# A hybrid encoder trunk: the attention and HGRN steps of its mixer are placed anew, and the Newton step of its inverse roots moves from VectorE to GpSimd

## The chip, the cores and the metric

The kernel runs on one core of a Trainium2 chip. What counts is the device time of one execution in microseconds (us). The engines are named as the profile names them: PE is TensorE (PEld its weight loads), DVE is VectorE, ACT is ScalarE, POOL is GpSimd and SP is SyncE, which here only issues DMAs. Each engine works through its own queue in order and waits on semaphores for the others.

## The reference

A two-layer trunk over 1024 tokens of width 1024, in float32. Layer 0 has a mixer of two head groups that share an input projection; layer 1 has a convolution module; each layer ends with a squared-ReLU MLP of width 4096, and an RMS norm stands before every block and at the end.

```python
u = rmsnorm(h, norm_mix_g[layer])
if layer % 2 == 0:
    h = h + parallel_ab_mixer(u, ...)      # stick-breaking attention (8 heads x 64) beside HGRN2 (4 heads x 128),
                                           # concatenated, one output projection
else:
    h = h + conformer_conv(u, ...)         # GLU, causal depthwise conv of width 31, LayerNorm, swish, pointwise
h = h + squared_relu_mlp(rmsnorm(h, norm_ffn_g[layer]), w_ff1[layer], w_ff2[layer])

# attention, per head: key_pos < q_pos
z = q @ k.T * scale;  log_beta = log_sigmoid(z);  log_keep = where(mask, log_beta - z, 0)
w = where(mask, exp(log_beta + cumsum_after(log_keep)), 0);  out = w @ v

# HGRN2, per head: f = lb + (1 - lb) * sigmoid(f_raw)
S_t = diag(f_t) S_{t-1} + (1 - f_t) i_t^T;  o_t = S_t^T q_t;  out = rmsnorm(o) * norm_g * silu(gate)

def rmsnorm(x, g):
    return x * rsqrt(mean(x * x) + 1e-6) * g
```

## The kernel before

The activations are kept transposed, channels on partitions and tokens along the free dimension, and are worked on in two halves of 512 tokens (`hf` 0 and 1, or a and b). A weight panel is 128 output channels by 1024 inputs: `panel` loads it by SP (`wraw`, two buffers) and splits it into a high part (ACT, line 104) and a low part (DVE, line 105); `gemm` then issues 24 matmuls of 128x512 for it (lines 115 to 117), three for each of eight input tiles, as high-high, high-low and low-high.

**The mixer's order is written by hand.** `TOKENS` lists the projection panels in order; each takes one place, from 0 up, except the tokens L, X, B, S and N, which take none. In the list, v, qk, f, q, i and g with a number and a half are projections; B loads the second half's input and S is its norm; X loads the residual `ht`; L4 and its like load one finished 128-channel block of the mixer's output back from DRAM on ACT's queue (`load_o`, into a `wraw` buffer); o0 to o7 are the output projection panels of the first half; N is the norm before the first MLP (`first_norm`); each m is one panel of that MLP. `A_SPANS` gives for each attention head the stretch of places over which its first and its second half's steps are spread evenly, and `G_SPANS` does so for the HGRN halves (entry 4 is head 2's first half, called 2a, entry 5 is 2b, entry 6 is 3a). `spread` sorts all steps by place and emits them in that order.

The emitted order is a priority, not yet the order on an engine: the framework's scheduler simulates the program and gives each engine the ready instruction of the highest priority. `tc.high_priority` puts panels' splits and evictions (`PRIO`) and the statistics (`SPRIO`) ahead. From there the order on each engine is fixed.

**An attention half** (`attn`) consists of `begin` (split of v), for each 128 queries `weights` (score matmuls with `kd` and `kl`, a sigmoid on ACT into `ke`, the mask on GpSimd at line 364, and a running product on DVE at line 367), for each pair of key blocks `apply` (transposes at line 380, a high/low split into `wt` on ACT and DVE at lines 384 and 385, and the product with v at line 389), and `end`, which writes the block to DRAM. A first half has nine steps and a second half thirteen. `ke` has three buffers, `wt`, `qs` and `kd` two or three, and the PSUM tags z, tr and av two each.

**An HGRN half** (`hg`) has seven steps: `gates` (a DVE scan, a reciprocal at line 460 and products), `level0` and two `level` steps, `state`, `output` (whose squares go through `stats`) and `finish`.

**`stats`** turns column sums of squares into 1/sqrt broadcast over partitions. TensorE sums (line 126), then a mean plus epsilon `m` is formed (line 129), GpSimd raises it to the power -0.5 (line 131), a Newton step refines it (lines 133 to 135), the result is split into high and low (137, 138), TensorE broadcasts it (`stb`, line 142) and ACT copies it out (144). It is called 21 times: for the norms, for the eight HGRN halves and for the LayerNorms.

After the mixer the rest of the second half's output projection, the MLPs, the convolution (31 taps on DVE, line 768) and layer 1 follow, with panels of the MLP interleaved with whatever DVE works on.

Of the kernel before, what the change touches and what calls it, by code (L numbers as in the profile page):

```python
# [8 lines left out]
F32 = mybir.dt.float32  # L9
F32R = mybir.dt.float32r  # L10
BF16 = mybir.dt.bfloat16
AF = mybir.ActivationFunctionType
ALU = mybir.AluOpType
# [14 lines left out]
TOKENS = (  # L28
# [4 lines left out]


A_SPANS = [
    (4, 7, 9.5, 12.5), (3, 8, 13, 13.2), (17, 18, 18, 20), (18.5, 21, 24, 29.5), (33, 33.2, 33.7, 35.5),
    (35, 36.5, 36.5, 36.7), (47, 48.5, 52, 66.5), (48.5, 48.7, 63, 74.5)
]
G_SPANS = [
    (4.5, 8), (18, 21.5), (23, 28), (28.5, 34.5), (38, 40), (49.5, 49.7), (40, 44), (65, 78)  # L40
]
GF = 8
XW = 2
# [10 lines left out]
def kernel(  # L54
# [13 lines left out]
    PE, ACT, DVE, POOL = nc.tensor, nc.scalar, nc.vector, nc.gpsimd  # L68
# [50 lines left out]
    def stats(pool, tag, src, count, eps, dst):  # L119

        n = dst.shape[-1] // P
        with tc.high_priority(offset=SPRIO):
            ps = pool.tile([P, H], F32, tag=tag, name="st")
            for c in range(n):
                for i, x in enumerate(src):
                    PE.matmul(ps[:, 2 * c:2 * c + 2], x[:, c * P:(c + 1) * P], ones[:, 0:2],  # L126
                              start=i == 0, stop=i == len(src) - 1, skip_group_check=True)
            m = tp.tile([P, 4], F32, tag="st_m", name="st_m")[:, :n]
            DVE.tensor_scalar(m, ps[:, 0:2 * n:2], 1.0 / count, eps, ALU.mult, ALU.add)
            r = tp.tile([P, 4], F32, tag="st_r", name="st_r")[:, :n]  # L130
            POOL.tensor_tensor(r, m, nhalf[:, :n], ALU.pow)
            t = tp.tile([P, 4], F32, tag="st_t", name="st_t")[:, :n]
            DVE.tensor_tensor(t, r, r, ALU.mult)
            DVE.scalar_tensor_tensor(t, t, -0.5, m, ALU.mult, ALU.mult)
            DVE.scalar_tensor_tensor(r, t, 1.5, r, ALU.add, ALU.mult)
            rr = tp.tile([P, 2, 4], F32R, tag="st_rr", name="st_rr")[:, :, :n]
            DVE.tensor_copy(rr[:, 0], r)
            DVE.tensor_tensor(rr[:, 1], r, rr[:, 0].bitcast(F32), ALU.subtract)
            pb = pool.tile([P, H], F32, tag=tag, name="stb")
            for c in range(n):  # L140
                for i in range(2):
                    PE.matmul(pb[:, c * P:(c + 1) * P], rr[:, i, c:c + 1].broadcast_to([P, P]), identr,  # L142
                              start=i == 0, stop=i == 1, skip_group_check=True)
            ACT.activation(dst, pb[:, :n * P], AF.Copy)
# [88 lines left out]
    with tc.high_priority(offset=PRIO):  # L233
        stats(pz, "tr", colsum_sq(lambda k: xs[0][k], two=True), D, 1e-6, rm0)

    def norm1():

        rm1 = wk.tile([P, H], F32, tag="ot", name="rm1", bufs=2)
        stats(pz, "tr", colsum_sq(lambda k: xs[1][k], two=True), D, 1e-6, rm1)
        u0[1] = scaled(lambda k: xs[1][k], V_MIX, rm1)  # L240
# [201 lines left out]
    def hg(hd, hf, dst):  # L442
# [95 lines left out]
        def output():  # L538
            qd, iv, before = hin[hd, "q", hf], hin[hd, "i", hf], L["before"]
            av = pz.tile([P, 4, P], F32, tag="av", name="ho")  # L540
            for c in range(4):
                PE.matmul(av[:, c], iv[:, c], L["sT"][:, c], start=True, stop=before[c] is None)
                if before[c] is not None:
                    PE.matmul(av[:, c], before[c], qd[:, c * P:(c + 1) * P], start=False, stop=True)
            L["av"] = av.rearrange("p c q -> p (c q)")
            sq = tp.tile([P, H], F32, tag="sq", name="hsq")
            ACT.activation(sq, L["av"], AF.Square)
            L["rh"] = wk.tile([P, H], F32, tag="ot", name="hrh", bufs=2)
            stats(pz, "tr", [sq], P, 1e-6, L["rh"])
# [150 lines left out]
    for name in TOKENS.split():  # L700
        f, n = name[0], name[1:]
# [14 lines left out]
        else:  # L716
            f, n, hf = name[:-2], int(name[-2]), "ab".index(name[-1])
# [108 lines left out]
    m = ms[0]  # L826
# [10 lines left out]
    m = mlp(0, 1, ub)  # L837
# [7 lines left out]
    m = mlp(1, 0, ua)  # L845
# [70 lines left out]
```

## Time and profile before

| | |
|---|---|
| median of 3 runs | 2303.07 us (2302.92 to 2303.27) |
| the profiled execution | 2305.74 us |
| its span, first to last instruction | 2304.0 us |
| mean granted clock of TensorE | 0.992 |
| PE busy | 2273.3 us, 99% |
| DVE busy | 1513.3 us, 66% |
| ACT busy | 886.3 us, 38% |
| POOL busy | 78.5 us, 3%, 145 instructions |

The profile comes from one execution. Busy times are sums of instruction durations over the span; matmuls are pipelined, so a busy TensorE may still be slowed by its clock, which is listed beside it as a share of full speed. A share over the whole span averages stages with different limits, so the stages are looked at one by one. In rows of groups the number after x is the count, then come busy time and mean duration in ns, then the idle time of the engine just before them and what ended it. In rows of the timeline come the start in us, the duration in us, the engine, the line, the operation and the tiles. In rows of waits stand the waiting instruction, the one waited for, then the total in us, how often, and the longest.

### The profile page before, as it was taken

What the parts mean: (1) busy time and instruction counts of PE and PEld (TensorE: products, weight loads), DVE (VectorE), ACT (ScalarE), POOL (GpSimd) and SP (SyncE); (2) the same over time, 40 slices, a digit from 0 to 9 for tenths busy, and PEclk for the clock granted to TensorE, in tenths of its full rate; (3) what the DMA queues carried; (4) which work ended last, traced back from release to release, by engine and by line L of the source; (5) the groups of instructions that cost most, each with busy time, mean ns of one, the idle gap of its engine ahead of it and who ended that gap; (6) DMA issues with size and microseconds to landing.
All of it is one profiled execution on the core that took longest, in us unless ns stands there. A gap on an engine that the chain in (4) does not pass through costs nothing.

```text
span 2304.0 us, 27457 instructions
## 1 busy us (share of the span) xinstructions
PE 2273.3 (99%) x10828; PEld 1906.4 (83%) x10828; DVE 1513.3 (66%) x2198; ACT 886.3 (38%) x1339; POOL 78.5 (3%) x145
## 2 busy tenths in 40 slices
PE   8999999999999999999999999999999999999998
PEld 7888887778888888888888888888888888888888
DVE  7787777657543453469999875799997546333344
ACT  6444344334433343342423363342324534342341
POOL 1110010100000000000000000000000000000000
PEclk9999999989999999999999999999999999999999
DMA  5221122232333232323233322333232333323241
GB/s 182 60 67 44 49 69 62 84 123 69 114 124 123 92 101 92 101 92 100 93 101 93 100 92 92 97 96 101 92 101 92 97 96 103 126 92 101 95 134 47
DMA packets 67345, 217.97 MB, mean 95 GB/s; under 512 B 7696, under 2 KB 9872, under 8 KB 67216
## 3 DMA queue, kind: packets, MB, share of 16 engines
q1 hardware_dynamic: 55296, 197.16, 27.1%
q10 hardware_dynamic: 10640, 16.96, 2.3%
q0 software_dynamic: 1280, 2.10, 0.4%
q8 instruction: 85, 1.39, 0.2%
q14 instruction: 44, 0.36, 0.1%
HBM read 205.70 MB, written 8.39 MB: 93 GB/s over the span
## 4 chain that ended last, share of the span: by engine, by line
PE 93%; issue 4%; DVE 2%; ACT 1%; DMA 0%; POOL 0%; POOLq 0%; DVEq 0%; ACTq 0%
PE mm L115 26%; PE mm L117 26%; PE mm L116 26%; PE av L389 1%; PE pa L115 1%; PE pg L115 1%; PE pg L116 1%; PE pa L117 1%; PE pa L116 1%; PE pg L117 1%; PE wtr L380 1%; PE zs L481 1%; PE st L126 1%; PE stb L142 1%; DVE ke L367 1%
## 5 line engine op out<-in xcount | busy, mean ns | idle before, releaser
L105 DVE TENSOR_TENSOR whl<-wraw,whl 128x1024 fp32r<-128x1024 f32 x364 | 444.9, 1223 | 321.0 <-ACT whl L104 320.5
L104 ACT ACTIVATE whl<-wraw 128x1024 fp32r<-128x1024 f32 x364 | 384.7, 1058 | 677.8 <-PE mm L117 527.9
L115 PE MATMUL mm<-u,whl 128*128 128x512 f32 x1456 | 572.0, 393 | 9.0 <-ACT u L229 6.8
L116 PE MATMUL mm<-u,whl 128*128 128x512 f32 x1456 | 571.5, 392 | 0.5 <-DVE u L230 0.5
L117 PE MATMUL mm<-u,whl 128*128 128x512 f32 x1456 | 571.6, 393 | 0.0
L115 PE MATMUL mm<-hid,whl 128*128 128x512 f32 (+1 forms) x1024 | 392.5, 384 | 0.0
L116 PE MATMUL mm<-hid,whl 128*128 128x512 f32 (+1 forms) x1024 | 391.9, 383 | 0.0
L117 PE MATMUL mm<-hid,whl 128*128 128x512 f32 (+1 forms) x1024 | 391.6, 383 | 0.0
L768 DVE SCALAR_TENSOR_TENSOR y<-a,vec,y 128x512 f32<-128x512 f32 x480 | 344.4, 746 | 4.2
L115 PEld LDWEIGHTS mm<-u,whl 128*128 128x128 f32 x1456 | 274.2, 188 | 64.3 <-ACT u L229 6.8
L116 PEld LDWEIGHTS mm<-u,whl 128*128 128x128 f32 x1456 | 274.3, 188 | 55.6 <-DVE u L230 1.0
L117 PEld LDWEIGHTS mm<-u,whl 128*128 128x128 f32 x1456 | 274.3, 188 | 55.0 <-issue 0.2
L116 PEld LDWEIGHTS mm<-hid,whl 128*128 128x128 f32 x1024 | 192.5, 188 | 37.5 <-issue 0.2
L117 PEld LDWEIGHTS mm<-hid,whl 128*128 128x128 f32 x1024 | 192.5, 188 | 37.4
L115 PEld LDWEIGHTS mm<-hid,whl 128*128 128x128 f32 x1024 | 192.5, 188 | 37.2 <-issue 0.2
L669 DVE TENSOR_TENSOR ht<-ht,mm 128x512 f32<-128x512 f32 x120 | 82.2, 685 | 198.1 <-PE mm L117 197.9
L651 ACT ACTIVATE relu<-mm 128x512 f32<-128x512 f32 x128 | 76.5, 598 | 328.8 <-PE mm L117 320.2
L367 DVE TENSOR_TENSOR_SCAN ke<-ke 128x128 f32<-128x128 f32 (+5 forms) x64 | 86.5, 1353 | 24.7 <-POOL ke L364 24.5
L654 DVE TENSOR_TENSOR hid<-sqr,hid 128x512 fp32r<-128x512 f32 x128 | 87.5, 683 | 13.4 <-ACT sqr L653 13.4
L653 ACT ACTIVATE sqr<-relu 128x512 f32<-128x512 f32 x128 | 79.6, 622 | 2.9 <-DVE hid L654 2.9
L652 ACT ACTIVATE hid<-relu 128x512 fp32r<-128x512 f32 x128 | 79.7, 623 | 0.3
L389 PE MATMUL av<-wt,vh 128*128 128x256 f32 (+1 forms) x320 | 63.3, 298 | 4.3 <-DVE wt L385 3.9
(205 smaller groups left out, 2454.6 us busy)
## 6 DMA issues: line engine op xcount, KB each, us to landing
wraw<-w_ff SPq DMA_DIRECT2D x257, 512.0 KB, 3.5
wraw<-w_in SPq DMA_DIRECT2D x47, 512.0 KB, 3.6
wraw<-w_glu SPq DMA_DIRECT2D x32, 512.0 KB, 3.5
wraw<-w_out SPq DMA_DIRECT2D x16, 512.0 KB, 3.6
wraw<-w_pw SPq DMA_DIRECT2D x16, 512.0 KB, 3.5
xk<-xT SPq DMA_DIRECT2D x16, 256.0 KB, 5.2
oraw<-o_dram ACTq DMA_DIRECT2D x16, 256.0 KB, 3.2
ht<-xT ACTq DMA_DIRECT2D x16, 256.0 KB, 3.8
```

The source lines that it names most:

```text
L104: ACT.activation(hi[:, :n], raw[:, :n], AF.Copy)
L105: DVE.tensor_tensor(lo[:, :n], raw[:, :n], hi[:, :n].bitcast(F32), ALU.subtract)
L115: PE.matmul(ps, whi[:, c], hi, start=start and k == 0, stop=False)
L116: PE.matmul(ps, whi[:, c], lo, start=False, stop=False)
L117: PE.matmul(ps, wlo[:, c], hi, start=False, stop=stop and k == n - 1)
L367: DVE.tensor_tensor_scan(kr, kr, kr, 1.0, ALU.mult, ALU.min)
L389: PE.matmul(live["av"][:, qo + o:qo + 256], vh[hd, (b0 + b) // 4][:, (b0 + b) % 4, :], wt[:, part, b * 256:b * 256 + 256 - o], start=start ...
L652: ACT.activation(hh[:, 0], t, AF.Square)
L653: ACT.activation(s, t, AF.Square)
L654: DVE.tensor_tensor(hh[:, 1], s, hh[:, 0].bitcast(F32), ALU.subtract)
L669: DVE.tensor_tensor(d, d, ps, ALU.add)
L768: DVE.scalar_tensor_tensor(y, a[:, j:j + H], w(j), y, ALU.mult, ALU.add)
```

## The change

It consists of three edits. `A_SPANS` of heads 4 to 7 and `G_SPANS` of halves 2a, 2b and 3a are set anew: the stretches of the heads' halves and of 2a and 2b become wider, and 2b moves from place 49.5 into the output panels at 52.5 to 58. In `TOKENS` the panel q3b moves from behind o7 to before L3 and the output panels, and i3b moves from behind N to before it. In `stats`, m goes from DVE to ACT, and the Newton step and the split go from DVE to GpSimd, where they take six instructions in place of DVE's five.

```diff
     "q1a qk3b i1b f1b i1a g1b g1a qk4a qk4b v2a v2b f2a q2a qk5a qk5b i2a f3a L4 q3a g2a i3a g3a qk7a "
-    "f2b qk6a v3a q2b i2b g2b L5 L6 qk6b L1 qk7b L2 v3b X L0 L7 L3 o5 o2 o0 o3 o4 o1 o6 o7 q3b N i3b "
+    "f2b qk6a v3a q2b i2b g2b L5 L6 qk6b L1 qk7b L2 v3b X L0 L7 q3b L3 o5 o2 o0 o3 o4 o1 o6 o7 i3b N "
     "f3b g3b m m m m m m m m m m m m m m m m ")
 A_SPANS = [
-    (4, 7, 9.5, 12.5), (3, 8, 13, 13.2), (17, 18, 18, 20), (18.5, 21, 24, 29.5), (33, 33.2, 33.7, 35.5),
-    (35, 36.5, 36.5, 36.7), (47, 48.5, 52, 66.5), (48.5, 48.7, 63, 74.5)
+    (4, 7, 9.5, 12.5), (3, 8, 13, 13.2), (17, 18, 18, 20), (18.5, 21, 24, 29.5), (31, 33, 33.5, 37),
+    (35.5, 37.5, 37.5, 41.9), (46.5, 49.5, 53, 66.5), (48.5, 51, 63, 74.5)
 ]
 G_SPANS = [
-    (4.5, 8), (18, 21.5), (23, 28), (28.5, 34.5), (38, 40), (49.5, 49.7), (40, 44), (65, 78)
+    (4.5, 8), (18, 21.5), (23, 28), (28.5, 34.5), (39, 42.5), (52.5, 58), (42.5, 46.5), (65, 78)
 ]
...
-            DVE.tensor_scalar(m, ps[:, 0:2 * n:2], 1.0 / count, eps, ALU.mult, ALU.add)
+            ACT.activation(m, ps[:, 0:2 * n:2], AF.Copy, scale=1.0 / count, bias=eps)
             r = tp.tile([P, 4], F32, tag="st_r", name="st_r")[:, :n]
             POOL.tensor_tensor(r, m, nhalf[:, :n], ALU.pow)
             t = tp.tile([P, 4], F32, tag="st_t", name="st_t")[:, :n]
-            DVE.tensor_tensor(t, r, r, ALU.mult)
-            DVE.scalar_tensor_tensor(t, t, -0.5, m, ALU.mult, ALU.mult)
-            DVE.scalar_tensor_tensor(r, t, 1.5, r, ALU.add, ALU.mult)
+            POOL.tensor_tensor(t, r, r, ALU.mult)
+            POOL.tensor_tensor(t, t, m, ALU.mult)
+            POOL.tensor_scalar(t, t, -0.5, 1.5, ALU.mult, ALU.add)
+            POOL.tensor_tensor(r, t, r, ALU.mult)
             rr = tp.tile([P, 2, 4], F32R, tag="st_rr", name="st_rr")[:, :, :n]
-            DVE.tensor_copy(rr[:, 0], r)
-            DVE.tensor_tensor(rr[:, 1], r, rr[:, 0].bitcast(F32), ALU.subtract)
+            POOL.tensor_copy(rr[:, 0], r)
+            POOL.tensor_tensor(rr[:, 1], r, rr[:, 0].bitcast(F32), ALU.subtract)
             pb = pool.tile([P, H], F32, tag=tag, name="stb")
```

## The prediction, made before the changed kernel ran

> **What bounds the kernel now.** I read the page first, then the waits of TensorE, then the busy time by stage, then which matmuls run inside the bad stages.
>
> ```profile
> PE 2273.3 (99%) x10828; PEld 1906.4 (83%) x10828; DVE 1513.3 (66%) x2198; ACT 886.3 (38%) x1339; POOL 78.5 (3%) x145
> ```
>
> TensorE is the bound: whatever the change does must show as less TensorE idle time or a better granted clock, because no matmul is added or removed. The stages tell where either is to be had (columns: stretch, its length, then busy us of PE, PEld, DVE, ACT, POOL, the granted clock, the DMA share, GB/s):
>
> ```profile
> 100.00:150.00 50.00, 50.00 (x263) 42.64 (x262) 39.88 (x56) 22.12 (x41) 5.26 (x11) 1.00 0.25 72
> ...
> 200.00:250.00 50.00, 50.00 (x298) 43.94 (x297) 36.12 (x64) 18.51 (x37) 3.36 (x8) 1.00 0.11 35
> ...
> 350.00:375.00 25.00, 20.62 (x106) 17.34 (x105) 20.90 (x30) 11.47 (x24) 3.17 (x6) 0.80 0.14 46
> 375.00:435.00 60.00, 60.00 (x334) 51.90 (x334) 40.08 (x81) 22.75 (x40) 4.23 (x8) 1.00 0.29 85
> 435.00:485.00 50.00, 43.33 (x199) 35.32 (x198) 34.87 (x66) 19.40 (x38) 8.07 (x12) 0.80 0.32 102
> 485.00:530.00 45.00, 45.00 (x215) 37.63 (x214) 25.63 (x30) 16.93 (x24) 0.32 (x1) 1.00 0.35 111
> 530.00:570.00 40.00, 39.81 (x208) 33.40 (x206) 29.64 (x46) 18.23 (x33) 2.52 (x4) 1.00 0.22 67
> ```
>
> Two stretches lose time, 350 to 375 us and 435 to 485 us: idle 25.00 - 20.62 = 4.38 and 50.00 - 43.33 = 6.67 us, and what ran there ran at a mean clock of 0.80, which costs 0.2 x 20.62 = 4.1 and 0.2 x 43.33 = 8.7 us. Together 8.5 + 15.4 = 23.9 us. DVE is the engine waited for, though it is no busier there (20.90 of 25, 34.87 of 50) than where TensorE never stops (39.88 of 50). What is missing is cover, as TensorE's panel matmuls in 350 to 375 us and their first rows in 375 to 435 us show (count, busy us, mean ns, idle before):
>
> ```profile
> L117 PE MATMUL mm<-u,whl 128*128 128x512 f32 x5 | 2.0, 392 | 0.0
> L116 PE MATMUL mm<-u,whl 128*128 128x512 f32 x5 | 2.0, 390 | 0.0
> L115 PE MATMUL mm<-u,whl 128*128 128x512 f32 x4 | 1.6, 412 | 0.0
> ```
> ```profile
> L117 PE MATMUL mm<-u,whl 128*128 128x512 f32 x65 | 25.8, 397 | 0.0
> ```
>
> Fourteen panel matmuls in 25 us against about 3 x 65 in 60 us. The rest of those 25 us is one attention chain (score, sigmoid, scan on DVE, transpose, split on DVE, product), and TensorE stands behind each DVE link. Who is waited for:
>
> ```profile
> PE av L389 <- DVE wt L385: 3.9, 4, 2.2
> PE wtr L380 <- DVE ke L367: 2.1, 6, 0.7
> PE mm L115 <- DVE qs L335: 2.0, 1, 2.0
> ...
> PE ho L544 <- DVE state L533: 1.7, 2, 1.4
> ```
>
> A stall also pays at the clock, as TensorE's timeline shows around the wait for qs:
>
> ```profile
> 439.48 0.39 PE L117 MATMUL mm<-u,whl 128*128 128x512 f32 x1
> 441.84 0.47 PE L115 MATMUL mm<-u,whl 128*128 128x512 f32 x1 [1.98 <-DVE qs L335]
> ...
> 444.84 0.63 PE L117 MATMUL mm<-u,whl 128*128 128x512 f32 x1
> 445.27 0.63 PE L115 MATMUL mm<-u,whl 128*128 128x512 f32 x1
> ...
> 446.02 0.39 PE L117 MATMUL mm<-u,whl 128*128 128x512 f32 x1
> 446.25 0.39 PE L115 MATMUL mm<-u,whl 128*128 128x512 f32 x1
> ```
>
> After 1.98 us of idle the matmuls take 0.63 us instead of 0.39 until about 445.9 us. The Trainium skill (TensorE: Matmul & The Clock Gate, "Part 1: The HAM clock gate") has the clock fall only after an idle window of about 3.4 us; by that rule this wait would cost no clock, and the trace disagrees.
>
> **The change, part by part.** *Spreading.* In the old order 46 attention and HGRN steps stand between the five panels at places 32 to 36 (13 of them, all of head 5's second half, at place 36) and 16 at places 48 and 49. In the new one places 30 to 41 hold 56 steps in 12 panels, at most 15 in any two, and head 7's first half and HGRN half 2b go over 2.5 and 5.5 panels. How much density is harmless? Places 17 to 20 hold 34 steps in four panels. They end with half 0b's output, whose statistics the timeline has here, in a stage with TensorE busy 50.00 of 50:
>
> ```profile
> 236.32 0.95 PE L126 MATMUL st<-ones,hsq 128*128 128x2 f32 x8
> ```
>
>  The new order is below that density throughout, so I count both stalled stretches as cured, except the qs wait: it came when DVE was inside half 2b's gates, and these move on with their block, to place 52, where they stand before the evictions of q3b and the first output panels. It keeps 1.98 us of idle and as much again at the measured 0.63 against 0.39 (about nine matmuls, start to start 0.43 instead of 0.23, 1.2 us), so 3.2. Gain 23.9 - 3.2 = 20.7 us.
>
> *Half 2b among the output panels.* Its largest DVE instruction is the reciprocal:
>
> ```profile
> L460 DVE RECIPROCAL hp<-hp 128x512 f32<-128x512 f32 x8 | 26.7, 3342 | 0.0
> ```
>
> With it come eight full-width passes (0.69 each, as L594's row below), seven of half that width and some 2.5 us of small ones: 3.3 + 5.5 + 2.5 + 2.5, an estimate of 14 us. They land in 485 to 530 us, where DVE is busy 25.63 of 45: they fit, at nothing. Without that cover it would be one more 3.2 us stall.
>
> *Panels q3b and i3b.* q3b moves ahead of L3 and the eight output panels; i3b moves ahead of N, the norm of the first MLP. Each takes its weight load on SP, its split on ACT and DVE, its PSUM bank and its eviction along. On SP q3b's 512 KB load passes eight w_out loads; L3's load on ACT's queue shares the two raw buffers and comes one panel later. What a load takes, by the page's row of DMA issues:
>
> ```profile
> wraw<-w_in SPq DMA_DIRECT2D x47, 512.0 KB, 3.6
> ```
>
> It lands in 3.6 us and a panel lasts 24 x 0.23 = 5.5 us, so I cost that at nothing. But between the last output panel and the first MLP panel stood q3b, i3b, f3b, g3b, and now only i3b, f3b, g3b. That cover is used now:
>
> ```profile
> 528.70 0.69 DVE L594 TENSOR_TENSOR ht<-ht,mm 128x512 f32<-128x512 f32 x1 [1.04 <-PE mm L117]
> ...
> 545.38 1.41 DVE L179 SCALAR_TENSOR_TENSOR un<-ht,vec,rbc 128x512 f32<-128x512 f32 x2 [1.43 <-ACT rbc L144]
> ...
> 566.30 0.67 DVE L163 TENSOR_TENSOR u<-un,u 128x512 fp32r<-128x512 f32 x1
> ```
>
> The norm needs 37.6 us from the last residual add to the last split of u, and the first MLP panel waits for that split while TensorE is busy 39.81 of 40. One panel less may cost nothing (the norm's DVE work is served earlier) or up to 5.5 us of idle, by the ratio of loss to idle above (23.9 / 11.05 = 2.2) 12 us in all. I take 3, a quarter: half of the 21.6 us between the first scaling and that split was other DVE work, which the scheduler may put behind.
>
> *The Newton step.* Per `stats` DVE loses six instructions (m and five after the power), ACT gains one, GpSimd six. The chain now, in an MLP stage, then beside a running DVE instruction, then at the end:
>
> ```profile
> 800.50 1.01 POOL L131 TENSOR_TENSOR st_r<-st_m,nhalf 128x4 f32<-128x4 f32 x1 [149.60 <-DVE st_m L129]
> 801.54 0.16 DVE L133 TENSOR_TENSOR st_t<-st_r 128x4 f32<-128x4 f32 x1 [1.12 <-POOL st_r L131]
> 802.34 0.16 DVE L138 TENSOR_TENSOR st_rr<-st_r,st_rr 128x4 fp32r<-128x4 f32 x1
> 806.99 1.00 PE L142 MATMUL stb<-identr,st_rr 128*128 128x128 f32 x8
> ...
> 1772.12 1.22 DVE L105 TENSOR_TENSOR whl<-wraw,whl 128x1024 fp32r<-128x1024 f32 x1
> 1772.28 1.92 POOL L131 TENSOR_TENSOR st_r<-st_m,nhalf 128x4 f32<-128x4 f32 x1 [92.34 <-DVE st_m L129]
> ...
> 2293.99 0.69 POOL L131 TENSOR_TENSOR st_r<-st_m,nhalf 128x2 f32<-128x2 f32 x1 [20.48 <-DVE st_m L129]
> 2294.71 0.16 DVE L133 TENSOR_TENSOR st_t<-st_r 128x2 f32<-128x2 f32 x1 [0.81 <-POOL st_r L131]
> 2295.61 0.85 PE L142 MATMUL stb<-identr,st_rr 128*128 128x128 f32 x4 [1.91 <-DVE st_rr L137]
> ```
>
> Five DVE links take 802.50 - 801.54 = 0.96 us. No row has a small multiplication on GpSimd; bounds are its cheapest small operation and the undisturbed power above (0.69):
>
> ```profile
> L759 POOL COPY a<-halo 128x30 f32<-128x30 f32 x8 | 3.2, 423 | 266.8 <-DVE y L768 266.8
> L756 POOL MEMSET a<- 128x30 f32 x8 | 1.0, 120 | 32.5 <-DVE y L768 21.0 <-DVE ht L669 11.4
> ```
>
> Six at 0.12 to 0.69 with 0.04 between them give 1.0 to 4.4 us; I take 0.3 each, under the copy of 30 columns, so 2.0 us, 1.1 us longer than now. In the body that is hidden: 802.50 to 806.99 leaves 4.5 us until TensorE takes the result. The last chain has no cover, so the end is 1.1 us later (0.0 to 3.4). The new wait of ACT on the statistics holds weight copies of later panels behind it, the new chain holds GpSimd's attention masks; ACT is 38% busy, GpSimd 3%: nothing. DVE gets back 21 x 1.0 us of links and the time it waits for the power, none of it counted.
>
> **Sum.** -20.7 + 3 + 1.1 = -16.6 us. The profiled execution took 2305.74 us (span 2304.0 and 1.7 around it), so it would be 2289.1; the median of the runs is 2303.07, 2.7 lower, and the same step gives 2286.5 us.
>
> **Rivals.** *Starved norm* (0.13): the missing panel costs its full 12 us instead of 3; 2295.5 us. For it speaks that the wait is just covered now; against, that the norm outranks the work it competes with. *One stretch only* (0.10): places set priorities, and a list scheduler decides; the second clump forms again around half 2b or head 7, and only 8.5 us come back: 2303.07 - 8.5 + 4.1 = 2298.7 us. *Nothing moves* (0.07): the same attention chains are bunched again because the schedule follows readiness, and the time is 2303 plus 1.1, 2304 us; against it, only 14 panel matmuls ran in a stretch whose priorities now hold a panel every five steps. *Slower* (0.10): GpSimd's links are held up by DVE. The 1.92 us power beside the 1.22 us L105 is 0.9 us over its 1.01; if each of six links pays that, the chain grows by 1.1 + 5.4 = 6.5 us, over the 4.5 us of slack by 2, in some 19 chains 38 us, less the 16.6: 2324 us. It decides once a link costs over (4.5 + 0.96) / 6 = 0.9 us, its gap included. The Trainium skill (GPSIMD Engine Reference, "1. Specifications") speaks for it: GpSimd shares SBUF interfaces with DVE and contends with DVE instructions of two SBUF inputs, and L105 is one. The 1.92 us row agrees. Against it: in MLP stages DVE has gaps, so few links meet such an instruction.
>
> **How the numbers follow.** The forecast, 2279 to 2294 us, has 0.60; its lower end is everything recovered and no new loss (2303.07 - 23.9). Below 2279 I see nothing of size. Leaving out the slower case, the upper part of "nothing moves" and a little at the bottom, the range is 2279 to 2303. A change within 0.2% (4.6 us) can hardly be told from none: under 2298.5 is faster (0.60 + 0.13 and half of "one stretch", 0.78), over 2307.7 slower (0.10), between them 0.12.
>
> **What would show it.** Right: TensorE busy all but about 2 us between 340 and 500 us, clock 1.00 there except after one wait, av and wtr waits gone, panel matmuls spread evenly; the last power to the last broadcast about 2.7 us instead of 1.6. Wrong: a TensorE wait on u just before the first MLP panel over 3 us; waits of stb on GpSimd; a new stretch at a clock near 0.8.

## The result, and the profile after

The changed kernel takes 2318.49 us (2318.14 to 2320.26), the kernel before in the same comparison 2303.17: a ratio of 1.0068 (1.0051 to 1.0086). It is slower by 15.3 us, where 2286.5 was forecast. The first row of the page, busy time by engine:

```profile
PE 2268.9 (98%) x10828; PEld 1902.2 (82%) x10828; DVE 1496.2 (65%) x2072; ACT 891.1 (38%) x1360; POOL 114.8 (5%) x271
```

TensorE is idle 2316.4 - 2268.9 = 47.5 us of the span, before 2304.0 - 2273.3 = 30.7. The extra 16.8 us of idle time is more than the 12.4 us that the span grew. The windows say where (stretch, length, busy us of PE, PEld, DVE, ACT, POOL, granted clock, DMA share, GB/s); the first five are the mixer stretches shown before:

```profile
350.00:375.00 25.00, 24.17 (x131) 19.72 (x131) 16.67 (x22) 13.04 (x24) 4.52 (x8) 1.00 0.27 81
375.00:435.00 60.00, 52.35 (x301) 45.35 (x299) 39.19 (x76) 19.84 (x40) 5.46 (x13) 0.94 0.16 47
435.00:485.00 50.00, 40.62 (x183) 33.30 (x184) 34.69 (x57) 21.79 (x35) 6.50 (x15) 0.83 0.43 142
485.00:530.00 45.00, 45.00 (x234) 38.35 (x233) 23.73 (x32) 16.57 (x27) 4.05 (x8) 1.00 0.27 88
530.00:570.00 40.00, 37.62 (x210) 31.77 (x208) 28.76 (x40) 17.73 (x33) 4.67 (x14) 1.00 0.23 73
570.00:600.00 30.00, 26.15 (x123) 21.56 (x124) 24.48 (x36) 14.62 (x26) 0.97 (x2) 0.94 0.29 84
```

The last stretch in the kernel before:

```profile
570.00:600.00 30.00, 30.00 (x144) 25.27 (x145) 20.24 (x31) 17.44 (x28) 0.69 (x2) 1.00 0.40 123
```

350 to 375 us is cured (0.83 us idle in place of 4.38, clock 1.00 in place of 0.80). But 375 to 435, which had no idle time, now has 7.65 us; 435 to 485 has 9.38 in place of 6.67; and 530 to 600, around the first MLP panel, has 2.38 + 3.85 in place of 0.19. Four places to look at.

**Behind the cured stretch.** The 25 us after it, first of the kernel before, then of the changed one:

```profile
375.00:400.00 25.00, 25.00 (x143) 21.80 (x143) 20.98 (x39) 9.85 (x16) 1.08 (x2) 1.00 0.22 56
```
```profile
375.00:400.00 25.00, 20.20 (x102) 16.79 (x100) 24.70 (x43) 8.90 (x16) 1.31 (x2) 0.88 0.15 42
```

DVE is busy 24.70 of 25 us, and TensorE waits five times for it or for what stands behind it. Over 350 to 400 us DVE does the same work as before (16.67 + 24.70 = 41.4 against 20.90 + 20.98 = 41.9); it lies later. The reciprocal of half 3a's gates starts at 385.61 us, before at 377.05, and now meets the second half of head 5 (line 368). Some of TensorE's waits, then DVE's rows around the longest instruction:

```profile
381.07 0.74 PE L390 MATMUL av<-wt,vh 128*128 128x128 f32 x4 [1.21 <-DVE wt L386]
...
395.25 1.10 PE L482 MATMUL zs<-hq,hf 128*128 128x64 f32 x8 [1.18 <-DVE hf L510]
397.37 1.22 PE L543 MATMUL ho<-sT,hi 128*128 128x128 f32 x4 [1.02 <-ACT sT L504]
```
```profile
385.27 0.42 DVE L460 TENSOR_SCALAR hf<-hf 128x512 f32<-128x512 f32 x1
385.61 3.34 DVE L461 RECIPROCAL hp<-hp 128x512 f32<-128x512 f32 x1
388.87 2.22 DVE L368 TENSOR_TENSOR_SCAN ke<-ke 128x1024 f32<-128x1024 f32 x1
391.01 0.66 DVE L386 TENSOR_TENSOR wt<-wtr,wt 128x512 fp32r<-128x512 f32 x1
```

No row in between names an idle reason: DVE goes from one instruction into the next.

**At 437 us** TensorE stands for the statistics of an HGRN half, and m, now on ACT, stands behind loads of X on ACT's queue (ACTq rows are those DMA issues):

```profile
432.28 1.05 PE L126 MATMUL st<-ones,hsq 128*128 128x2 f32 x8 [0.69 <-ACT hsq L548]
437.03 0.47 PE L143 MATMUL stb<-identr,st_rr 128*128 128x128 f32 x1 [3.70 <-POOL st_rr L138]
```
```profile
433.43 0.88 ACTq L604 DMA_DIRECT2D ht<-xT  x1
434.35 0.17 ACT L129 ACTIVATE st_m<-st 128x4 f32<-128x4 f32 x1 [2.13 <-issue]
```

**In the first output panel** TensorE waits twice for the panel's weights. The first wait is for the high part, on ACT; ahead of the low part (line 105) DVE's rows show the gates of half 2b, without a gap:

```profile
471.60 0.50 PE L115 MATMUL mm<-ou,whl 128*128 128x512 f32 x1 [2.04 <-ACT whl L104]
477.33 0.80 PE L117 MATMUL mm<-ou,whl 128*128 128x512 f32 x1 [5.00 <-DVE whl L105]
```
```profile
470.25 1.23 DVE L455 TENSOR_TENSOR_SCAN hp<-hf,hp 128x512 f32<-128x512 f32 x1
...
472.78 3.35 DVE L461 RECIPROCAL hp<-hp 128x512 f32<-128x512 f32 x1
476.05 0.10 DVE L469 TENSOR_TENSOR tots<-tots 128x8 f32<-128x8 f32 x1
476.07 1.21 DVE L105 TENSOR_TENSOR whl<-wraw,whl 128x1024 fp32r<-128x1024 f32 x1
```

**Around the first MLP panel** the norm is now late (the wait for u), and attention steps wait for DVE as well (ke and wt):

```profile
565.59 0.44 PE L381 MATMUL wtr<-ident,ke 128*128 128x128 f32 x2 [1.48 <-DVE ke L368]
571.07 0.50 PE L116 MATMUL mm<-u,whl 128*128 128x512 f32 x1 [1.08 <-DVE u L164]
575.21 1.22 PE L390 MATMUL av<-wt,vh 128*128 128x256 f32 x4 [2.49 <-DVE wt L386]
```

### The profile page after: what moved, and what is told of

The parts are those of the page before. It is cut to its first block, busy times and chain, and to the rows that moved or that the text cites. A ratio compares the mean times of both kernels' runs of the same rounds, so it can differ in the third digit from the quotient of the medians.

```text
span 2316.4 us, 27506 instructions
## 1 busy us (share of the span) xinstructions
PE 2268.9 (98%) x10828; PEld 1902.2 (82%) x10828; DVE 1496.2 (65%) x2072; ACT 891.1 (38%) x1360; POOL 114.8 (5%) x271
## 3 DMA queue, kind: packets, MB, share of 16 engines
q8 instruction: 85, 1.39, 0.2%
## 4 chain that ended last, share of the span: by engine, by line
PE 94%; DVE 3%; DMA 1%; issue 1%; ACT 1%; POOL 0%; ACTq 0%; DVEq 0%; POOLq 0%
PE mm L117 26%; PE mm L115 26%; PE mm L116 26%; PE pa L115 1%; PE pg L116 1%; PE pa L117 1%; PE pa L116 1%; PE pg L115 1%; PE pg L117 1%; PE av L390 1%; PE wtr L381 1%; PE zs L482 1%; PE st L126 1%; PE stb L143 1%; DMA oraw<-o_dram 1%
## 5 line engine op out<-in xcount | busy, mean ns | idle before, releaser
L131 POOL TENSOR_TENSOR st_r<-st_m,nhalf 128x4 f32<-128x4 f32 (+1 forms) x21 | 25.6, 1221 | 1219.0 <-ACT st_m L129 1219.0
```

## The experiments

All ratios are to the kernel before, run on the same chip (2302.0 to 2303.1 us there), with 95% intervals. "New places" means the new `TOKENS`, `A_SPANS` and `G_SPANS` with the Newton step left on DVE.

**The two halves of the change.**

```diff
 newton_only:  kernel before, stats() from the changed one
 places_only:  changed kernel, stats() from the one before
```

> Kernel before with only the statistics changed (mean on ACT, Newton step and split on GpSimd); all places old. Theory 'places' (the stalls were moved by the new places, the Newton move costs little): the changed kernel's extra idle time in 0 to 100 us (12.0 against 9.1 us, where no place differs) and the longer end come from this part, so about 2303 + 2.9 + 0.9 = 2307 us. Rival 'Newton' (the mean behind ACT's queue and the longer GpSimd chain hold TensorE wherever statistics are taken): 2313 us or more, with stb waits over 5 us.

> Kernel before with only the new places (TOKENS, A_SPANS, G_SPANS); Newton step on DVE as before. Theory 'places': the first 300 us as before, the rest of the loss stays, about 2303 + 12 = 2315 us, with idle time before the first output panel and before the first MLP panel (about 560 us). Rival 'Newton': the forecast holds for the places alone, 2285 to 2292 us. Third possibility, the parts do not add (each gives a new static order): the two parts' differences sum to something else than +15 us by over 5 us.

Measured: newton_only 2301.51 us, ratio 0.9994 (0.9984 to 1.0003); places_only 2315.83, 1.0056 (1.0039 to 1.0073). The places make nearly all of the loss; the Newton step by itself, at the old places, costs nothing that can be told from nothing.

**The places in parts.**

```diff
 heads_2a_3a:   before + A_SPANS new, G_SPANS entry 4 (38, 40) -> (39, 42.5), entry 6 (40, 44) -> (42.5, 46.5)
 half_2b_only:  before + G_SPANS entry 5 (49.5, 49.7) -> (52.5, 58)
 old_panels:    new places, TOKENS of before
 q3b_moved:     new places, i3b behind N as before
 i3b_moved:     new places, q3b behind o7 as before
```

> Only the spans of heads 4 to 7 and of HGRN halves 2a and 3a are new; half 2b and all panels stay at their old places; Newton step on DVE. If the wider heads cure the stretch at 350 to 375 us as forecast and only the moved half and panels hurt: 2303 - 8.5, 2290 to 2296 us. If the heads' stalls only move on (the changed kernel idles 5.6 us in 350 to 400 us against 4.4): 2301 to 2306 us.

> Kernel before with one entry changed: HGRN half 2b at places 52.5 to 58 instead of 49.5 to 49.7; Newton step on DVE. The runs so far: new heads with 2b in its old place +15.8 us, the same with 2b moved -0.1 us. If the parts add, moving 2b is worth about -16 us by itself: 2286 to 2291 us, and the stretch at 435 to 485 us loses its 15.4 us. If 2b's move only repairs what the wide heads broke (head 7's first half beside 2b), it is within 4 us of before.

> All spans new, half 2b among the output panels, but the panel list is the old one (q3b and i3b behind the output panels and behind N); Newton step on DVE. Against the run with all places this tells what the two panels do. If the missing panel before the first MLP panel starves it, as the trace at 560 to 578 us says (6.2 us idle and its clock), this is 8 to 12 us below the run with all places. If that stall has another cause: within 3 us of it.

> All new spans and panel q3b before the output panels, but i3b behind N as before; Newton step on DVE. Against all new spans with old panels (2302.4) and with both panels moved (2315.8). If q3b is the cover that is missing before the first MLP panel and its weight load pushes the first output panel's: 2313 to 2317 us. If i3b's place (ahead of the norm N) does the harm: 2301 to 2305 us.

> All the new spans, Newton on DVE, of the two panels only i3b moved ahead of the last norm; q3b stays where it was. If the two prices add (9.7 for q3b, 3.7 for i3b after it): 2305 to 2307, with a norm ahead of the MLP that starves by 1.5 to 4 us and no wait on the output panels' weights over 1 us. Rival (i3b costs nothing by itself, the 3.7 came from what q3b left): 2301 to 2303.5.

| kernel | median us | ratio |
|---|---|---|
| heads_2a_3a | 2318.34 | 1.0069 (1.0054 to 1.0084) |
| half_2b_only | 2302.54 | 1.0001 (0.9992 to 1.001) |
| old_panels | 2302.44 | 1.0001 (0.9992 to 1.001) |
| q3b_moved | 2312.1 | 1.004 (1.0025 to 1.0055) |
| i3b_moved | 2307.75 | 1.0021 (1.0012 to 1.003) |

Spans alone don't add: wide heads lose 16 us, the new span of 2b gives nothing by itself, together they are at nothing. A span is only a priority, and with the old panels 2b's gates hardly follow theirs. Their reciprocal starts at 435.13 us in the kernel before, at 438.90 in half_2b_only and here in old_panels, then in q3b_moved:

```profile
436.95 3.34 DVE L460 RECIPROCAL hp<-hp 128x512 f32<-128x512 f32 x1
```
```profile
469.77 3.35 DVE L460 RECIPROCAL hp<-hp 128x512 f32<-128x512 f32 x1
```

So half_2b_only moves a label, and it is q3b's new place that sends the gates to the output panels. Why they have to wait there was not isolated. So all new spans with the old panels win nothing: the time from 350 to 375 us is lost again behind it, as in old_panels' two windows:

```profile
350.00:375.00 25.00, 23.87 (x127) 19.50 (x126) 18.62 (x26) 13.78 (x25) 4.60 (x8) 1.00 0.32 95
375.00:400.00 25.00, 20.24 (x111) 17.20 (x110) 24.61 (x43) 9.45 (x17) 0.82 (x2) 0.86 0.13 37
```

On top of that the two panels do add, roughly: by the ratios q3b costs 0.0039 x 2303 = 9.0 us and i3b 0.0020 x 2303 = 4.6, together 13.6, against 12.7 for both. q3b_moved has the wait of 5.03 us on whl in the first output panel, i3b_moved has no wait on the output panels' weights, and one of 3.4 us on u ahead of the first MLP panel.

**Is it DVE?** These two runs leave out the reciprocal of the gates and put a cheap instruction (0.41 us instead of 3.34) in its place.

```diff
-            DVE.reciprocal(pp, pp)
+            DVE.tensor_scalar(pp, pp, -1.0, 2.0, ALU.mult, ALU.add)
```

> Left out: the reciprocal in every HGRN half's gates (2 - p stands in its place, 0.41 instead of 3.34 us on DVE); all new places, Newton step on DVE. Theory 'DVE blocks' (the new stalls at 375 to 400, at the first output panel and before the first MLP panel each have a DVE that is full around a half's gates, whose reciprocal cannot be interrupted): 2.9 us less in three stalls with their clock, 2315.8 - 10 to 16, 2299 to 2306 us, and the distance to the old places without the reciprocal under 5 us. Rival (too few panels between the steps, whatever DVE costs): over 2311 us.

> Left out: the same reciprocal, in the kernel before; old places. It is the reference for the run above. 'DVE blocks': the old places gain less than the new ones, since only the qs wait at 440 us stands behind a reciprocal: 2297 to 2302 us. Rival: both gain alike, about 2303 less what the run above gains.

places_cheap_gates: 2297.39, 0.9976 (0.9967 to 0.9986); before_cheap_gates: 2294.72, 0.9966 (0.9953 to 0.9978). The new places win 18.4 us by it, the old ones 7.5 to 7.8, and of the 13.3 us between the two 2.7 are left. So most of the difference between the places hangs on the gates. Stalls are left all the same: in places_cheap_gates TensorE is idle 1.39 us in 375 to 400 (4.76 in places_only), but 3.80 in 400 to 425 and 6.98 in 450 to 475. Three readings remained: one instruction of 3.34 us blocks others, the amount of DVE work is too high, or the chain inside one half is too long.

**One block or the amount?**

```diff
-            DVE.reciprocal(pp, pp)
+            for c in range(4):
+                DVE.reciprocal(pp[:, c * P:(c + 1) * P], pp[:, c * P:(c + 1) * P])
```

> The new places with the Newton step left on DVE, and the reciprocal of the gates cut into four pieces of 128x128. The work on DVE is the same or a little more; only one block of 3.34 us becomes four of some 0.85 us, between which the static order can put other instructions. Theory A (the block itself holds up the others: what waits behind a running reciprocal is late by up to 3.34 us): the waits of 5.02 us on the ACT weights of the first output panel and of 3.33 us ahead of the first MLP panel shrink to about 1 to 2.5 us, and the time falls by 4 to 9 us against the new places with whole reciprocals (2315.8), to 2307 to 2312. Theory B (it is the amount of DVE work in 375 to 400 and 450 to 475 us, full to 24.7 of 25 us): cutting it frees nothing, 2314 to 2318, and DVE stays at 24.5 or more of 25 in 375 to 400.

> The kernel before with the reciprocal of the gates cut into four pieces of 128x128, nothing else. Theory A: the stalls at 350 to 375 (4.38 us) and 450 to 500 (4.69 us) shrink by some 1 to 3 us together with their slow clock: 2297 to 2301. Theory B: no change, 2301 to 2305. It is also the yardstick for the same cut at the new places.

> All the new spans of heads and halves, the old order of panels, Newton on DVE, the reciprocal cut in four. It has the panels' covers back (2302.4 with whole reciprocals). Theory A: the waits left at 375 to 400 and 425 to 450 us (4.76 and 4.85) shrink by a quarter to a half, 2296 to 2300, faster than both kernels. Theory B: 2301 to 2304.

Measured: 2316.11, 1.0057 (1.004 to 1.0073); 2302.93, 1.0003 (0.9994 to 1.0012); 2301.23, 0.9997 (0.9988 to 1.0006). None gains, and the wait on whl in places_split_recip is 5.3 us. But in the stalls in question the cut did not break the block. DVE runs the four pieces one behind the other, at 382.94 us and here ahead of the first output panel's weights:

```profile
468.58 3.38 DVE L461 RECIPROCAL hp<-hp 128x128 f32<-128x128 f32 x4
471.87 0.10 DVE L469 TENSOR_TENSOR tots<-tots 128x8 f32<-128x8 f32 x1
471.89 1.21 DVE L105 TENSOR_TENSOR whl<-wraw,whl 128x1024 fp32r<-128x1024 f32 x1
```

So these runs say nothing against the single block: that reading stays untested.

**The amount or the chain?** Two instructions of the gates, 1.1 us per half, leave DVE, while the half's own chain gets longer.

```diff
-            DVE.tensor_tensor(qd, qd, pp, ALU.mult)
+            POOL.tensor_tensor(qd, qd, pp, ALU.mult)
...
-            DVE.tensor_scalar(ff, ff, -1.0, 1.0, ALU.mult, ALU.add)
+            ACT.activation(ff, ff, AF.Copy, scale=-1.0, bias=1.0)
```

> The kernel before, with two full-width instructions of every half's gates taken off DVE: hq times hp (0.68 us) goes to GpSimd, one minus hf (0.43 us) to ACT. The results are the same. Theory (amount of DVE work decides): a third of what the cheap reciprocal took away, so about a third of its 7.5 us, 2299 to 2301. Rival (the longer chain through three engines costs what the room brings, or GpSimd's 128x512 product takes several us beside DVE): 2302 to 2306.

> All the new spans, the old order of panels, Newton on DVE, and the same two instructions of the gates off DVE. Theory (amount of DVE work decides): 2296 to 2300, below both kernels, with DVE below 24 of 25 us in 375 to 400 and less idle PE there than 4.76 us. Rival: 2301 to 2305.

> The new places with Newton on DVE, and hq times hp on GpSimd (0.68 us on DVE before, 1.55 us there) and one minus hf on ACT, of every half's gates. DVE loses 1.1 us per half, but the chain of one half's gates gets longer. Theory A (what the cheap reciprocal gave back at the new places, 18.4 us for 2.9 us less per half, came from less DVE work): a third of it or so, 4 to 9 us, 2307 to 2312. Theory B (it came from the shorter chain of the half itself): no gain or a loss, 2314 to 2320.

> The old places, the Newton step on GpSimd and m on ACT as in the change, and the two instructions of the gates off DVE: both reliefs of DVE together. If they add: 2299.4 from the gates and 0 to 1.5 less from the Newton step, 2297.5 to 2300, the fastest of all kernels here with the full computation. Rival (GpSimd's 1.55 us products stand ahead of the statistics' links, and the late norm costs): 2300 to 2305.

| kernel | median us | ratio |
|---|---|---|
| before_gates_off_dve | 2299.36 | 0.9983 (0.9974 to 0.9992) |
| old_panels_gates_off_dve | 2300.77 | 0.9994 (0.9984 to 1.0004) |
| places_gates_off_dve | 2311.78 | 1.0037 (1.0024 to 1.005) |
| newton_and_gates_off_dve | 2300.25 | 0.9988 (0.998 to 0.9997) |

DVE was not relieved by it. Its busy time is 1513.4 us in before_gates_off_dve (1513.3 in the kernel before) and 1514.2 in places_gates_off_dve (1513.1 in places_only): the 8 x 1.1 us that left come back as longer instructions, above all in the copy of 32 columns in line 458, here in the kernel before and in before_gates_off_dve:

```profile
L458 DVE COPY hf<-hp 128x32 f32<-128x32 f32 x8 | 1.6, 202 | 0.0
```
```profile
L458 DVE COPY hf<-hp 128x32 f32<-128x32 f32 x8 | 4.8, 603 | 0.0
```

One of these copies takes 1.26 us, from 464.28 us in places_gates_off_dve, while GpSimd's product runs from 464.23 to 465.49. At the new places 4.0 us come back (2315.83 to 2311.78; the two kernels' runs do not meet, 2309.3 to 2312.9 and 2314.7 to 2316.4, though their ratios' intervals do). But the old places gain as much: by the ratios the new places lose 0.0056 against the old ones with the gates whole and 0.0054 with the two instructions moved. So these runs show a small gain of another kind, whose cause is open, and they can't tell the amount from the chain. before_gates_off_dve is faster than both kernels; the Newton step on GpSimd adds nothing to it, and the intervals of the two overlap. In places_gates_off_dve, behind the same gates, TensorE stands longer than ever in 450 to 475 us, for half 2b's own chain, with DVE busy 19 of 25 us (window, then the wait):

```profile
450.00:475.00 25.00, 15.18 (x74) 12.26 (x74) 19.19 (x36) 9.14 (x15) 2.44 (x3) 0.84 0.20 54
```
```profile
PE zs L481 <- DVE hf L489: 8.9, 1, 8.9
```

The mean misleads: during the wait itself, 463.1 to 471.9 us, DVE is never idle. It works through the gates of half 2b, with 1.17 us of attention (line 407) between them. So the chain of one half on DVE holds TensorE there, which has nothing else to do in its fixed order.

**Half 2b later, and m back on DVE.**

```diff
 places_2b_late:     new places, G_SPANS entry 5 (52.5, 58) -> (55.5, 60)
 after_mean_on_dve:  changed kernel, line 129 on DVE as before
```

> The new places with Newton on DVE, half 2b at (55.5, 60) in place of (52.5, 58). Theory A (the price of q3b among the output panels is that the gates of half 2b, 7.9 us of DVE without a break at 466.5 to 474 us, stand ahead of the second weight conversion of the first output panel): three places on, the gates meet another panel with another panel's work to cover them; the wait of 5.02 us on whl goes below 1.5 and the time falls by 4 to 8 us, to 2308 to 2312. Theory B (the panels behind have no room wherever the half stands): a wait of 3 to 6 us of the same kind shows further on, by 485 to 500 us, and the time stays at 2313 to 2318.

> The changed kernel with one line put back: the mean m is formed on DVE again, while the Newton links stay on GpSimd. Theory A (m on ACT sits behind eight loads of X on its queue at 428.6 to 434.4 us, which makes the waits of 3.70 on stb and the 4.88 us of idle PE at 425 to 450): that idle time falls to about the 3.3 us of the new places with Newton on DVE, and the time to about 2316. Rival (the difference between the changed kernel and the new places alone is a different static order, or the links on GpSimd): no change, 2317.5 to 2319.5, and stb still waits over 3 us there.

places_2b_late: 2311.7, 1.0036 (1.0023 to 1.005). The wait of 5 us on whl is gone, and the first output panel keeps 1.80 us on ACT's part; 4.1 us come back. But the stretch ahead of the MLP has 6.19 us of idle time in place of 5.33 in places_only, DVE busy 24.84 of 25:

```profile
550.00:575.00 25.00, 18.81 (x90) 15.39 (x91) 24.84 (x43) 10.88 (x22) 1.38 (x2) 0.80 0.20 59
```

So the phase of half 2b against that panel is some 4 of q3b's 9 us. That the rest lies ahead of the MLP is likely, not shown: in 550 to 575 us q3b_moved has 5.10 us of idle time, old_panels 2.17. after_mean_on_dve: 2319.68, 1.0075 (1.006 to 1.009), no gain. The wait of stb falls from 3.7 to 2.7 us, so ACT's queue makes 1.0 us of it, and the time doesn't follow: my theory on m falls as far as the time goes.

## Why the prediction was wrong, point by point

- **Both stretches cured, -20.7: the step that failed.** "The new order is below that density throughout, so I count both stalled stretches as cured" counted steps per panel. A step is no unit: one `gates` step holds 3.34 us of reciprocal and some 4 us of other DVE work, a `weights` step of a second half a scan of up to 2.3. The yardstick (places 17 to 20) was chosen by count as well. What the runs showed in its place: the term measured nothing (old_panels, 2302.44 against 2302.52). 350 to 375 is cured, as forecast, and 4.8 us of idle time stand 25 us later, where DVE is full. In old_panels the second stretch falls from 6.67 to 3.03 us of idle time, but 375 to 435 us has 8.08 and 530 to 570 has 2.17, where 0 and 0.19 stood. The rival "one stretch only" (2298.7) was nearer in its mechanism, and still too good: with the old panels the spans come to nothing, and the clump behind (4.76 us idle in 375 to 400) is as large as the first was (4.38).
- **Half 2b among the output panels, "at nothing".** It was right that DVE has room on average (23.73 of 45 us in 485 to 530). But the gates don't land there. With the old panels they stay at 437 us; with q3b ahead they run in one go at 470 us, ahead of the low part of the first output panel's weights: 5.00 us of wait. (The 2.04 us just before are ACT's, and 1.80 of such a wait is left when 2b goes later in places_2b_late.) The prediction named "one more 3.2 us stall" for the case without cover, idle time and clock together; here the idle time alone is 5.00.
- **q3b and i3b, +3: the other term that failed.** Costing q3b by its load alone was wrong: its price is 9.0 us, some 4 of it through the phase of half 2b. i3b costs 4.6. Together they are some 13 us, over the 12 named as the upper end. The mechanism of the starved norm was named and sized at 3; in i3b_moved the wait on u is 3.39 us, in the changed kernel waits on u, wtr and av stand at 560 to 575 us.
- **The new wait of ACT, "nothing".** 2.13 us idle ahead of m at 434.35, DMA issues among it, worth 1.0 us of the stb wait. The time did not show it.
- **The Newton step, +1.1: right.** The last chain:

```profile
2305.56 0.71 POOL L131 TENSOR_TENSOR st_r<-st_m,nhalf 128x2 f32<-128x2 f32 x1 [18.92 <-ACT st_m L129]
2306.35 0.19 POOL L133 TENSOR_TENSOR st_t<-st_r 128x2 f32<-128x2 f32 x1
...
2307.67 1.18 PE L143 MATMUL stb<-identr,st_rr 128*128 128x128 f32 x4 [2.46 <-POOL st_rr L138]
2307.70 0.20 POOL L139 TENSOR_TENSOR st_rr<-st_r,st_rr 128x2 fp32r<-128x2 f32 x1
2308.89 0.38 ACT L145 ACTIVATE rbc<-stb 128x256 f32<-128x256 f32 x1 [3.40 <-PE stb L143]
```

  The six links take 2307.90 - 2306.35 = 1.55 us (2.0 forecast, five on DVE 0.96), and from the end of TensorE's last sum to the broadcast's copy it is 3.67 us, before 2.79: +0.9. In the body newton_only shows no loss.
- **The slower rival, through GpSimd's links: the right side for the wrong reason.** The slowest link of the 19 chains of four columns has a mean of 427 ns, far from the 0.9 us from which it would have decided (a single one took 1.93 us):

```profile
L135 POOL TENSOR_SCALAR st_t<-st_t 128x4 f32<-128x4 f32 x19 | 8.1, 427 | 1.7
L133 POOL TENSOR_TENSOR st_t<-st_r 128x4 f32<-128x4 f32 x19 | 4.4, 234 | 1.4
```

- **The clock.** The prediction priced an idle us at about two, since the clock falls with it. Between the two profiled executions that does not hold: 16.8 us more idle time, 12.4 us more span, and a mean clock of 0.992 in both. But the one of the kernel before took 2305.74 us, 2.6 over its median, and in later comparisons its runs near 2303 us have a clock of 0.994. Against the medians it is 15.3 us, still far under two for one. Matmuls do run slow behind the new stalls (last section); why the sum is smaller than the idle time was not isolated.

Put together: the spans brought nothing in place of -20.7, the two panels some +13 in place of +3, the Newton step at the old places nothing that can be told in place of +1.1.

**What stays open.** Whether the 2.7 us between places_only and the changed kernel is real (the intervals of the two ratios overlap); in newton_only as in the changed kernel the first 100 us have over 2 us more idle time (12.05 against 9.14 before in the changed one), yet newton_only's time does not show it. And by what the gates hold TensorE: one block, the amount of DVE work or the chain of one half. No run here separates the three. For the stall at 375 to 400 us as well it is open how much is DVE's amount and how much the fixed order: in places_gates_off_dve its idle time falls only from 4.76 to 3.38 us with DVE still busy 24.29 of 25.

## What to carry to other kernels

Where a list of steps is spread by hand, weigh each step by its work on the engine waited for, stage by stage, and look 25 us past the stretch that is to be cured: work that leaves a clump lands somewhere. A panel moved out of a stretch takes its cover along, so ask what was hidden under it at both ends, and place a long chain of vector work away from the first panel of a new stage. Taking two instructions of the gates off DVE (to engines 3% and 38% busy) won 3.9 us at the old places, which no new order of the same work did; since DVE's busy time did not fall, why it helped is not known. And read in the trace whether an edit reached the engine: here four pieces still ran as one block, two instructions less left DVE as busy as before, and a new span left its gates where they were.

## What the runs showed of the hardware that was not expected

- The clock fell without one long idle time. In places_2b_late TensorE waits 1.80 us, runs two matmuls, waits 0.80 us, and from 473.05 us on eight panel matmuls take 0.63 us in place of 0.39 (two of them shown):

```profile
469.02 0.50 PE L115 MATMUL mm<-ou,whl 128*128 128x512 f32 x1 [1.80 <-ACT whl L104]
469.36 0.40 PE L116 MATMUL mm<-ou,whl 128*128 128x512 f32 x1
470.56 1.33 PE L380 MATMUL wtr<-ident,ke 128*128 128x128 f32 x5 [0.80 <-DVE ke L367]
...
473.48 0.63 PE L116 MATMUL mm<-ou,whl 128*128 128x512 f32 x1
...
475.61 0.63 PE L115 MATMUL mm<-ou,whl 128*128 128x512 f32 x1
```

- A reciprocal of 128x512 on DVE takes 3.34 us, the one-input pass of line 459 413 ns; cut into four pieces of 0.91 us, which overlap, it takes 3.38. The Trainium skill (VectorE: DVE Perf Modes, "First, the fixed hardware budget") has the reciprocal as a divide repeated eight times; the trace fits that (3.34 / 0.413 = 8.1).
- A GpSimd product of 128x512 takes a mean of 1.55 us, 2.3 times DVE's 681 ns; the median of the eight is 1.32 us, 1.9 times, and one took 3.19. The Trainium skill (GPSIMD Engine Reference, "4.1 Engine selection") puts operations of two inputs at about twice DVE's time; the median agrees:

```profile
L457 POOL TENSOR_TENSOR hq<-hq,hp 128x512 f32<-128x512 f32 x8 | 12.4, 1552 | 45.4 <-DVE hp L454 30.2 <-issue 15.1
```

- GpSimd's small links take 0.19 to 0.20 us where nothing disturbs them, close to DVE's 0.16; the links of the Newton chain lose 0.6 us by the move (1.55 against 0.96).
- While such a product runs, a small DVE instruction can take as long as the product: the copy of 32 columns above took 1.26 us in place of 0.19. Another, at 190.03 us of the same run, took 0.19 us beside the product, so it is not always so.
